# A hybrid attention and gated-MLP layer in float32 splits: where squares, first loads, a gate and a residual are placed

## Chip, cores, metric

One core of one Trainium2 chip runs the whole layer in one launch. The metric is the device time of a run in microseconds (us), median over runs. TensorE is PE in the profile, VectorE DVE, ScalarE ACT, GpSimd POOL, and SyncE (SP) issues the DMAs.

## What is computed

One layer over 1024 positions of width 1024. `mod` comes from a small product of the conditioning vector and gives shift, scale and gate for both halves.

```python
h = modulate(rmsnorm(x, g_attn_norm[l]), sh_a, sc_a)
proj = jnp.dot(h, w_in[l])
...
o_mla = mla_attention(q, k, v)
...
o_ca = chunk_attention(cq, ck, cv, rel_bias[l])
mixed = jnp.dot(jnp.concatenate([o_mla, o_ca], axis=-1), w_out[l])
x = x + g_a[:, None, :] * mixed
h = modulate(rmsnorm(x, g_mlp_norm[l]), sh_m, sc_m)
u = causal_dwconv(jnp.dot(h, w_up[l]), conv_w[l], conv_b[l])
gate, val = jnp.split(u, 2, axis=-1)
x = x + g_m[:, None, :] * jnp.dot(jax.nn.silu(gate) * val, w_down[l])
```

All inputs are float32. `w_up` is 1024 x 5632 (gate and value columns), `w_down` 2816 x 1024.

## The kernel before

**Splits.** To multiply float32 on TensorE each operand is split into a high part (a rounded copy, mostly by ScalarE, `hi_of`, L75) and a low part (operand minus high part, `lo_of`, L82, or L1098 for the up weights). A product is then three matmuls: high x high, high x low, low x high. Matmuls are 128 x 128 by 128 x 512.

**Order.** The kernel is written on a framework that places tiles in pools, sets the semaphores, and fixes each engine's order of instructions beforehand with estimated times: an instruction goes in when its inputs and its buffer are expected to be ready, earlier lines of the program first. At run time every engine, and SyncE's queue of DMA issues, goes strictly in that order. `tc.issue_after(ins)` puts the instructions of its block behind `ins` on the same engine.

**Attention (to about 695 us).** Scores, softmax and values of 32 units, with projections woven in as fillers. The last filler, `f_oca` (L689), takes the chunk attention's half of the output projection: for each half n of the columns it loads four blocks of `w_out` (`load_wo`, L677), splits them, and for eight tiles t of positions loads the attention output, multiplies (tile `oc`), copies PSUM to an SBUF tile `co` (L701, ScalarE) and stores it to `part_d` in DRAM. `co`, the raw blocks `wor` and others share two buffers ("sq"). `f_ada` (L503) makes the modulation vectors on the side; the attention gate, spread over 128 partitions, goes to `ga_d`.

**Output projection (about 695 to 785).** `load_wo` brings the other half's weights (L1022). First the up weights of tiles 0 and 1 are loaded and scaled (L1124 to L1127). Then for each t (L1129): load `ol`, split it (ScalarE, GpSimd), load x and the kept part `pa`, multiply (tile `op`), then on VectorE pa + op, times the gate row `gabc`, plus x (L1143 to L1145); x1 is stored to `x1_d`, squared (ScalarE), and scaled in place by its inverse root mean square (GpSimd for t < 4, else ScalarE). After t = 3 the first half of the positions is transposed and modulated (`mod_T`, L1048) and split into pages (`bpage`, L1056); the second half follows after the first products of tiles 0 and 1 (`ff_first`).

**Up stage (about 785 to 1259).** 22 tiles j of 128 gate and 128 value columns. The product of the two weight blocks with the two halves of the positions is done in seven products instead of eight, by sums and differences of blocks (`ff_w`, L1109, gives the split weights wa to wg in turn; `ff_tile`, L1195, multiplies and recombines in tile `c`). Each product is 12 matmuls in float16 parts; so that the parts keep within range, a tile's raw weights (`wu`, 8 buffers, four tiles) are first squared and summed on ScalarE (L1083), summed over partitions by TensorE (L1085), and scaled (L1093): `scale_ff`, L1078. `conv` (L1175) is the depthwise convolution: one ScalarE and two VectorE instructions each for gate and value; then SiLU, the product of both (L1222) and a store to `g_d` (L1223). The loop (L1272 on) calls for tile j: load of tile j+3, scaling of tile j+2, the seven products of j, and one step of `gate_row`, which makes the MLP gate `gmbc`.

**Down stage (from about 1259).** For each half h of the positions all eight PSUM banks hold 4 x 2 output tiles. The four x1 tiles are loaded (`xo`, L1308); for each j the block of `w_down` is loaded (`wd`), multiplied by the gate (L1313) and split, g is loaded (`gr`, L1316) and split, and 24 matmuls (L1323 to L1325) accumulate. At the end VectorE adds x1 (L1329) and the result is stored.

```python
    for j in range(NF):
        if j + 3 < NF:
            load_ff(j + 3)
        if j + 2 < NF:
            scale_ff(j + 2, bank("G", f"wss_ps{j + 2}"))
        ff_tile(j)
        if j >= 2:
            next(gate, None)
```

Of the kernel before, what the change touches and what calls it, by code (L numbers as in the profile page):

```python
# [12 lines left out]
F32 = mybir.dt.float32  # L13
# [49 lines left out]
def layer_kernel(ctx, tc, I, out):  # L63
# [9 lines left out]
    def hi_of(eng, o, i):  # L73
        if eng == "a":
            act.activation(o, i, AF.Copy)  # L75
        elif eng == "p":
            pool.tensor_scalar(o, i, 1.0, 0.0, op0=MUL, op1=ADD)  # L77
        else:
            dve.tensor_copy(o, i)
# [22 lines left out]
    pool.memset(nhalf[:], -0.5)  # L102
    modT = cst.tile([P, 4, ND], F32, name="modT")
# [399 lines left out]
    def f_ada():  # L503
        for m in (2, 3, 4):
            for n in range(4):
# [15 lines left out]
                if m == 2:  # L521
# [3 lines left out]
                    sp.dma_start(ga_d[:, n * 256:(n + 1) * 256], g[:])  # L525
                else:
# [150 lines left out]
    def load_wo(k0, n, he, le):  # L677
        ws = []
        for k in range(k0, k0 + 4):
            raw = qtile(f"wor{k}_{n}")  # L680
            sl = slice(n * 512, (n + 1) * 512)
            sp.dma_start(raw[:], I["w_out"][k * P:(k + 1) * P, sl])
            w = g4([P, 2, 512], F32R, f"wo{k}_{n}")
            hi_of(he, w[:, 0], raw[:])
            lo_of(le, w[:, 1], raw[:], w[:, 0])
            ws.append(w)
        return ws

    def f_oca():  # L689
        for n in range(2):  # L690
            ws = load_wo(4, n, "a", "p")
            for t in range(NT):
# [8 lines left out]
                act.activation(o[:], pt[:], AF.Copy)  # L701
# [230 lines left out]
    ca_done = []  # L932

# [131 lines left out]
    gabc = gb.tile([P, D], F32, name="gabc")  # L1065
    sp.dma_start(gabc[:], ga_d[:])


    raws, wsc = {}, {}
# [8 lines left out]
    def scale_ff(j, pt):  # L1078
        t = cst.tile([P, 4], F32, name=f"wss{j}", tag="wss", bufs=3)
        sv = cst.tile([P, 2, 4], F32, name=f"wcv{j}", tag="wcv", bufs=3)  # L1080
        for i in range(2):
            junk = xp.tile([P, D], BF16, name=f"wj{i}_{j}", tag="wj", bufs=1)
            act.activation(junk[:], raws[j][i][:], AF.Square, accum_out=t[:, i:i + 1])  # L1083
        for i in range(2):
            pe.matmul(pt[:, 0:1], ones[:], t[:, i:i + 1], start=(i == 0), stop=(i == 1))  # L1085
        dve.tensor_scalar(t[:, 2:3], pt[:, 0:1], 1.0 / VSCALE ** 2, 1e-20, op0=MUL, op1=ADD)
        pool.tensor_tensor(t[:, 2:3], t[:, 2:3], nhalf[:], op=ALU.pow)
        dve.reciprocal(t[:, 3:4], t[:, 2:3])
# [6 lines left out]
    def split(src, nm):  # L1095
        w = mt("ws", [P, 2, 512], nm, F16)
        hi_of("a", w[:, 0], src)
# [30 lines left out]
    gens = {}  # L1128
    for t in range(NT):  # L1129
        lo = gb.tile([P, 4, P], F32R, name=f"ol{t}", tag="ol", bufs=3)  # L1130
        hi = gb.tile([P, 4, P], F32R, name=f"oh{t}", tag="oh", bufs=3)
        sp.dma_start(f32(lo[:]), oT_d[0:4, :, t * P:(t + 1) * P].rearrange("k p t -> p k t"))
        hi_of("a", hi[:], f32(lo[:]))
        lo_of("p", lo[:], f32(lo[:]), hi[:])
        x1 = tb.tile([P, D], F32, name=f"x1_{t}", tag="x1", bufs=8)
        sp.dma_start(x1[:], I["x"][t * P:(t + 1) * P, :])
        pa = gb.tile([P, D], F32, name=f"pa{t}", tag="pa", bufs=3)
        sp.dma_start(pa[:], part_d[t])
# [8 lines left out]
        act.activation(pa[:], x1[:], AF.Square, accum_out=ss2[:, t:t + 1])  # L1147
        rsqrt_mean(r2[:, t:t + 1], ss2[:, t:t + 1], D)
        xn2[t] = x1
        if t < 4:  # L1150
            scale_pool(x1[:], x1[:], r2[:, t:t + 1])
        else:
# [41 lines left out]
    def ff_tile(j):  # L1194
# [28 lines left out]
        sp.dma_start(g_d[j], ug[:])  # L1223

    w0 = [next(gens[0]) for _ in range(2)]
# [19 lines left out]
    tbp.__exit__(None, None, None)  # L1245
# [159 lines left out]
```

## Time and profile before

| | |
|---|---|
| median of 3 runs | 1528.38 us (1525.49 to 1531.11) |
| profiled execution | 1528.33 us, its span 1526.6 us |
| mean granted TensorE clock | 0.939 |
| busy share of the span | PE 87%, DVE 69%, ACT 53%, POOL 47% |
| moved by DMA | 153.05 MB, mean 100 GB/s |

The span runs from the first to the last instruction on the core. A row of the timeline gives start (us), duration, engine, line, operation, tiles written and read, shapes, count, and in brackets the idle time before it with what ended it. A row of waits gives who waited for whom, us in total, times, and the longest. The letter q behind an engine's name means its queue, "x8" that eight instructions are merged. A matmul's duration includes its fill; the distance between two starts is what it costs in a row of many.

### The profile page before, as it was taken

The numbers are of one execution on the slowest core, as the hardware profiler recorded it, in microseconds if no ns is written. First come the engines' busy times: TensorE is split into PE (matmuls) and PEld (weight loads), VectorE is DVE, ScalarE is ACT, GpSimd is POOL, SyncE is SP. The second block draws the span as 40 slices with busy tenths as digits, with TensorE's granted clock in tenths as the row PEclk, the third lists the DMA queues.
The fourth block names the chain that finished last, engine by engine and source line by source line (L and its number), as shares of the span: only waits on it lengthen the run. The fifth ranks groups of instructions, "written<-read, shape, count | busy, mean of one in ns | idle before, by whom it ended". The sixth has DMA issues, their size and how long they took to land. (4 is left out here: it accounts for less than half of the span.)

```text
span 1526.6 us, 20386 instructions
## 1 busy us (share of the span) xinstructions
PE 1328.3 (87%) x7016; PEld 902.0 (59%) x7016; DVE 1054.8 (69%) x1721; ACT 814.7 (53%) x1537; POOL 717.3 (47%) x753
## 2 busy tenths in 40 slices
PE   3779999988888899977879899888898994999999
PEld 2679878867655466645634344433344443888887
DVE  8856776665898755575459986786777975656654
ACT  5445565455777677666277654555456422333332
POOL 5543342333353433224722865554555623665764
PEclk9879999999889899988889999999999996999999
DMA  8322123211100133228332322211221006445442
GB/s 304 107 81 64 55 83 107 82 56 44 54 22 12 49 94 99 82 63 310 112 138 76 118 84 83 83 70 55 83 81 44 39 32 264 142 146 198 153 147 96
DMA packets 82308, 153.05 MB, mean 100 GB/s; under 512 B 8470, under 2 KB 44570, under 8 KB 82204
## 3 DMA queue, kind: packets, MB, share of 16 engines
q1 hardware_dynamic: 82204, 151.75, 29.6%
q8 instruction: 55, 0.90, 0.2%
q14 instruction: 49, 0.40, 0.1%
HBM read 122.88 MB, written 28.84 MB: 99 GB/s over the span
## 5 line engine op out<-in xcount | busy, mean ns | idle before, releaser
L82 POOL TENSOR_TENSOR wds<-wd,wds 128x512 fp32r<-128x512 f32 x88 | 156.0, 1792 | 118.9 <-ACT wds L75 118.9
L1323 PE MATMUL dn<-wds,g 128*128 128x512 f32 x352 | 135.7, 395 | 22.1 <-ACT g L75 22.1
L75 ACT ACTIVATE wds<-wd 128x512 fp32r<-128x512 f32 x88 | 54.8, 624 | 164.9 <-PE dn L1325 146.6
L1324 PE MATMUL dn<-wds,g 128*128 128x512 f32 x352 | 136.5, 391 | 0.0
L1325 PE MATMUL dn<-wds,g 128*128 128x512 f32 x352 | 134.8, 389 | 0.0
L1313 DVE TENSOR_TENSOR wd<-wd,gmbc 128x1024 f32<-128x1024 f32 x44 | 68.9, 1566 | 90.4 <-DMA wd<-w_down 90.4
L1083 ACT ACTIVATE wj<-wu 128x1024 bf16<-128x1024 f32 x44 | 46.4, 1054 | 110.4 <-DMA wu<-w_up 103.4
L1177 ACT ACTIVATE u<-c,pk,wcv 128x1024 f32<-128x1024 f32 x44 | 52.1, 1232 | 70.4 <-DVE c L1217 49.6
L1323 PEld LDWEIGHTS dn<-wds,g 128*128 128x128 f32 x352 | 67.1, 191 | 36.7 <-ACT g L75 22.6
L515 DVE SCALAR_TENSOR_TENSOR aacc<-aw,cs,aacc 128x256 f32<-128x256 f32 x84 | 45.2, 538 | 56.6 <-DMA aw<-w_ada 56.2
L82 DVE TENSOR_TENSOR g<-gr,g 128x512 fp32r<-128x512 f32 x44 | 72.8, 1655 | 12.4 <-ACT g L75 12.3
L839 PE MATMUL tm<-qt,kt 96*128 96x512 f16 (+7 forms) x288 | 75.3, 351 | 6.2 <-ACT qt L802 3.6
L850 DVE TENSOR_TENSOR hlm<-pm,hlm 128x512 f16<-128x512 f32 (+1 forms) x96 | 55.2, 581 | 36.8 <-ACT hlm L847 18.9
L1098 POOL TENSOR_TENSOR wd<-wu,wd 128x512 f16<-128x512 f32 x22 | 40.4, 1835 | 85.1 <-issue 66.5
L1324 PEld LDWEIGHTS dn<-wds,g 128*128 128x128 f32 x352 | 66.7, 189 | 13.8
L1325 PEld LDWEIGHTS dn<-wds,g 128*128 128x128 f32 x352 | 66.2, 188 | 13.8
L843 ACT ACTIVATE pc<-tc,sca 128x512 f32<-128x512 f32 (+3 forms) x96 | 49.9, 522 | 38.3 <-DVE hlc L850 20.5
L77 POOL TENSOR_SCALAR hlm<-pm 128x384 f16<-128x384 f32 (+2 forms) x48 | 24.4, 509 | 97.2 <-ACT pm L843 74.8
L1121 DVE TENSOR_TENSOR wu<-wu 128x512 f32<-128x512 f32 x22 | 26.0, 1181 | 60.9 <-POOL wb L1098 60.6
L839 PEld LDWEIGHTS <-kt 128*128 128x128 f16 (+2 forms) x480 | 47.1, 102 | 35.2 <-issue 16.6
L1178 DVE SCALAR_TENSOR_TENSOR u<-c,wcv,u 128x1023 f32<-128x1023 f32 x44 | 57.4, 1340 | 12.2 <-ACT u L1177 12.2
L843 ACT ACTIVATE pm<-tm,scm 128x512 f32<-128x512 f32 (+1 forms) x96 | 55.2, 578 | 19.1 <-PE tm L839 15.3
(463 smaller groups left out, 4605.8 us busy)
## 6 DMA issues: line engine op xcount, KB each, us to landing
wu<-w_up SPq DMA_DIRECT2D x44, 512.0 KB, 3.8
wd<-w_down SPq DMA_DIRECT2D x44, 512.0 KB, 3.6
aw<-w_ada SPq DMA_DIRECT2D x96, 128.0 KB, 2.1
g_d<-u SPq DMA_DIRECT2D x22, 512.0 KB, 2.6
gr<-g_d SPq DMA_DIRECT2D x44, 256.0 KB, 3.7
x<-x SPq DMA_DIRECT2D x16, 512.0 KB, 10.1
adaw<-w_ada_a SPq DMA_DIRECT2D x16, 512.0 KB, 4.5
wq_r<-w_qk SPq DMA_DIRECT2D x32, 128.0 KB, 2.4
```

The source lines that it names most:

```text
L75: act.activation(o, i, AF.Copy)
L82: return (pool if eng == "p" else dve).tensor_tensor(o, i, f32(hi), op=SUB)
L839: last = pe.matmul(s[:, c0:c1], l, m, start=(y == 0), stop=(y == len(todo) - 1))
L843: act.activation(p[:, :w], s[:, :w], AF.Exp, scale=ninv)
L850: dve.tensor_tensor(hl[:, 1, :w], p[:, :w], hl[:, 0, :w], op=SUB)
L1083: act.activation(junk[:], raws[j][i][:], AF.Square, accum_out=t[:, i:i + 1])
L1177: act.activation(u[:], c, AF.Identity, scale=sv[:, 2:3], bias=pk[:, C_CV + 4 * ch + 3:C_CV + 4 * ch + 4])
L1178: dve.scalar_tensor_tensor(u[:, 1:], c[:, :S - 1], sv[:, 1:2], u[:, 1:], op0=MUL, op1=ADD)
L1313: dve.tensor_tensor(raw[:], raw[:], gmbc[:], op=MUL)
L1323: pe.matmul(pts[t][n], sh, w[n][:, 0], start=(j == 0), stop=False)
L1324: pe.matmul(pts[t][n], sh, w[n][:, 1], start=False, stop=False)
L1325: pe.matmul(pts[t][n], sl, w[n][:, 0], start=False, stop=(j == NF - 1))
```

## The change

It has five parts. (1) In the up stage a tile's weights are squared behind the last high part split so far, which is a tile two back, since `scale_ff` now follows `ff_tile`; the store of g of tile j-1 is issued in iteration j, behind the load of tile j+3; the square root's inverse and the root itself are both made by GpSimd. (2) The first three loads of `w_down` and of g are issued in the last three iterations of the up stage, into a pool of their own (`dna`), and the down stage's other buffers are opened in the up stage's place; its PSUM banks are taken in another order; x1 is loaded at steps 4 to 7; 3 buffers for gr instead of 5. (3) The gate of the attention is multiplied into the output weights, and the residual x is added in the kept part, so the output projection has one sum left. (4) In the output projection, four tiles' loads go first, the low part of `ol` and the scaling are VectorE's, and the first up weights are loaded and scaled between the tiles. (5) All pages of the first half have their low part made by VectorE.

```diff
+                    if n == 3:
+                        ga_done.append(1)
...
             sp.dma_start(raw[:], I["w_out"][k * P:(k + 1) * P, sl])
+            pool.tensor_tensor(raw[:], raw[:], gab[0][:, sl], op=MUL)
...
     def f_oca():
+        while not ga_done:
+            next(side[0])
+        gab.append(pgtile([P, D], F32, "gabc"))
+        sp.dma_start(gab[0][:], ga_d[:])
...
-                act.activation(o[:], pt[:], AF.Copy)
+                sp.dma_start(o[:], I["x"][t * P:(t + 1) * P, n * 512:(n + 1) * 512])
+                dve.tensor_tensor(o[:], o[:], pt[:], op=ADD)
                 sp.dma_start(part_d[t][:, n * 512:(n + 1) * 512], o[:])
...
+    def behind(x):
+        return tc.issue_after(x.ins) if x is not None else nullcontext()
...
-        for i in range(2):
-            junk = xp.tile([P, D], BF16, name=f"wj{i}_{j}", tag="wj", bufs=1)
-            act.activation(junk[:], raws[j][i][:], AF.Square, accum_out=t[:, i:i + 1])
+        with behind(last.get("hi")):
+            for i in range(2):
+                junk = xp.tile([P, D], BF16, name=f"wj{i}_{j}", tag="wj", bufs=1)
+                act.activation(junk[:], raws[j][i][:], AF.Square, accum_out=t[:, i:i + 1])
...
+        pool.tensor_tensor(t[:, 3:4], t[:, 2:3], phalf[:], op=ALU.pow)
         pool.tensor_tensor(t[:, 2:3], t[:, 2:3], nhalf[:], op=ALU.pow)
-        dve.reciprocal(t[:, 3:4], t[:, 2:3])
...
     def split(src, nm):
         w = mt("ws", [P, 2, 512], nm, F16)
-        hi_of("a", w[:, 0], src)
+        last["hi"] = hi_of("a", w[:, 0], src)
...
-    for j in range(2):
-        load_ff(j)
-    for j in range(2):
-        scale_ff(j, ps2.tile([P, 512], F32, name=f"wss_ps{j}", tag="hT", bufs=2))
+    def load_o(t):
+        lo = gb.tile([P, 4, P], F32R, name=f"ol{t}", tag="ol", bufs=4)
+        hi = gb.tile([P, 4, P], F32R, name=f"oh{t}", tag="oh", bufs=4)
+        sp.dma_start(f32(lo[:]), oT_d[0:4, :, t * P:(t + 1) * P].rearrange("k p t -> p k t"))
+        x1 = tb.tile([P, D], F32, name=f"x1_{t}", tag="x1", bufs=8)
+        sp.dma_start(x1[:], part_d[t])
+        o_hl[t] = hi, lo
+        xn2[t] = x1
+
+    for t in range(4):
+        load_o(t)
+        if t % 2:
+            load_ff(t // 2)
     for t in range(NT):
...
+        if t + 4 < NT:
+            load_o(t + 4)
...
-        lo_of("p", lo[:], f32(lo[:]), hi[:])
+        lo_of("v", lo[:], f32(lo[:]), hi[:])
...
-        dve.tensor_tensor(pa[:], pa[:], pt[:], op=ADD)
-        dve.tensor_tensor(pa[:], pa[:], gabc[:], op=MUL)
-        dve.tensor_tensor(x1[:], x1[:], pa[:], op=ADD)
+        dve.tensor_tensor(x1[:], x1[:], pt[:], op=ADD)
         sp.dma_start(x1_d[t], x1[:])
...
-        if t < 4:
-            scale_pool(x1[:], x1[:], r2[:, t:t + 1])
-        else:
-            act.activation(x1[:], x1[:], AF.Copy, scale=r2[:, t:t + 1])
+        dve.tensor_scalar(x1[:], x1[:], r2[:, t:t + 1], None, op0=MUL)
+        if t == 1:
+            scale_ff(0, ps2.tile([P, 512], F32, name="wss_ps0", tag="hT", bufs=2))
         if t == 3:
             for k in range(ND):
                 mod_T(k, 0, ps2, "hT", 2)
-                bpage("b11" if k < 4 else "b21", k % 4, hf[k, 0], "v" if k % 2 else "p")
-            gens[0] = iter(list(ff_w(0)))
+                bpage("b11" if k < 4 else "b21", k % 4, hf[k, 0], "v")
+            gens[0] = ff_w(0)
+            w0 = [next(gens[0]) for _ in range(2)]
+        if t == 4:
+            gens[0] = iter(list(gens[0]))
+            scale_ff(1, ps2.tile([P, 512], F32, name="wss_ps1", tag="hT", bufs=2))
...
-        sp.dma_start(g_d[j], ug[:])
+        gout.append((j, ug))
...
+    def store_g():
+        while gout:
+            j, ug = gout.pop(0)
+            sp.dma_start(g_d[j], ug[:])
...
+    def load_down():
+        h, j = steps[len(dl)]
+        raw = dna.tile([P, D], F32, name=f"wd{h}_{j}", tag="wd", bufs=3)
+        last["wd"] = sp.dma_start(raw[:], I["w_down"][j * P:(j + 1) * P, :])
+        gr = dna.tile([P, 512], F32, name=f"gr{h}_{j}", tag="gr", bufs=3)
+        sp.dma_start(gr[:], g_d[j][:, h * 512:(h + 1) * 512])
+        dl.append((raw, gr))
...
             load_ff(j + 3)
+        if j >= NF - 3:
+            load_down()
+        store_g()
+        ff_tile(j)
         if j + 2 < NF:
             scale_ff(j + 2, bank("G", f"wss_ps{j + 2}"))
-        ff_tile(j)
...
+        for t, n in ((0, 0), (0, 1), (1, 0), (3, 0), (3, 1), (1, 1), (2, 0), (2, 1)):
+            pts[t][n] = ps4.tile([P, 512], F32, name=f"dn{t}{n}_{h}", tag=f"d{t}{n}", bufs=1)[:]
...
+            if len(dl) <= h * NF + j:
+                load_down()
+            raw, gr = dl[h * NF + j]
...
+            if h == 0 and j == 0:
+                store_g()
+            if j in (4, 5, 6, 7):
+                t = j - 4
+                xo.append(dnb.tile([P, D], F32, name=f"xo{h}{t}", tag="xo", bufs=5))
+                with behind(last["wd"]):
+                    sp.dma_start(xo[t][:], x1_d[4 * h + t])
```

More of the change, by code (lines that the diff above doesn't have):

```diff
@@ L1 @@
 import math
-from contextlib import ExitStack
+from contextlib import ExitStack, nullcontext
 import numpy as np
@@ L102, in layer_kernel @@
     pool.memset(nhalf[:], -0.5)
+    phalf = cst.tile([P, 1], F32, name="phalf")
+    pool.memset(phalf[:], 0.5)
     modT = cst.tile([P, 4, ND], F32, name="modT")
@@ L932, in layer_kernel @@
     ca_done = []
+    ga_done = []
     def fill_step():
@@ L1222, in ff_tile @@
         dve.tensor_tensor(ug[:], ug[:], uv[:], op=MUL)
-        sp.dma_start(g_d[j], ug[:])
-    w0 = [next(gens[0]) for _ in range(2)]
+        gout.append((j, ug))
+    gout = []
+    def store_g():
+        while gout:
+            j, ug = gout.pop(0)
+            sp.dma_start(g_d[j], ug[:])
     ff_first(0, w0, "p27")
@@ L1270, in layer_kernel @@
     gate = gate_row()
+    dl = []
+    steps = [(h, j) for h in range(2) for j in range(NF)]
+    def load_down():
[5 more added lines that the diff above has]
+        dl.append((raw, gr))
     load_ff(2)
```

63 lines of the change are left out of this document (23 added, 40 removed).

## The prediction

> **What bounds the kernel now.** I read the stages first (busy time by stretch, cut where TensorE changes its work): 694.7 is the end of attention, 784.7 the second half of the transposes, 812.5 the first full tile of the up stage, 1258.7 its last product, 1280.8 the first product of the down stage. Columns: stretch, length, busy us (instructions) of PE, PEld, DVE, ACT, POOL, then granted clock, DMA share, GB/s.
>
> ```profile
> 694.70:716.80 22.10, 19.49 (x80) 15.45 (x80) 8.01 (x12) 12.26 (x20) 7.68 (x9) 0.92 0.93 350
> 716.80:735.40 18.60, 3.99 (x8) 1.83 (x8) 12.01 (x11) 9.82 (x17) 18.43 (x14) 0.57 0.62 226
> 735.40:784.70 49.30, 45.44 (x193) 31.32 (x194) 24.43 (x20) 23.03 (x37) 25.53 (x27) 0.89 0.36 128
> 812.50:900.00 87.50, 79.71 (x357) 35.87 (x357) 80.43 (x86) 57.18 (x84) 60.01 (x39) 0.94 0.32 106
> 900.00:1180.00 280.00, 250.19 (x1154) 114.29 (x1153) 199.00 (x194) 153.61 (x221) 142.46 (x114) 0.98 0.20 72
> 1180.00:1258.70 78.70, 74.65 (x333) 33.18 (x331) 65.19 (x56) 31.68 (x43) 38.91 (x29) 0.96 0.08 34
> 1258.70:1280.80 22.10, 0.02 (x1) 0.02 (x1) 9.61 (x8) 5.10 (x6) 1.04 (x1) 0.57 0.57 213
> 1280.80:1526.60 245.80, 242.00 (x1056) 199.88 (x1056) 146.69 (x103) 76.91 (x129) 154.91 (x88) 0.99 0.46 159
> ```
>
> The down stage is TensorE's own: 1056 matmuls in 245.8 us (0.233 each, tail included) at clock 0.99, so only what lies before it can be had. TensorE loses 14.6 us in one hole at 716.8, 22.1 between up and down, and in the up stage more than its busy time shows, because after each wait the clock is down for some us. The waits of the up stage (812 to 1260: total us, times, longest), then SyncE's own queue, and from the page's DMA issues the w_up loads (KB, median us to landing):
>
> ```profile
> ACT wj L1083 <- DMA wu<-w_up: 98.5, 26, 8.6
> DVE wu L1121 <- POOL wb L1098: 58.5, 14, 6.6
> PE p L1105 <- DVE c L1211: 29.1, 11, 4.0
> SPq L1223 <- DVE u L1222: 345.6, 22, 21.2
> ...
> wu<-w_up SPq DMA_DIRECT2D x44, 512.0 KB, 3.8
> ```
>
> The rows link into a ring, read from the last wait of PE back. The second product (L1211's p27 buffer is single) waits for VectorE; VectorE is late because L1121 sits ahead of L1217 and waits for GpSimd's low part of wb; that waits for ScalarE's high part; ScalarE stands in the squares of L1083, at the head of its queue, waiting for a weight load; and the load stands in SyncE's queue behind the store of g, which waits for the previous tile's last VectorE product L1222. The timeline shows the ring's pace.
>
> ```profile
> 1067.72 0.38 PE L1105 MATMUL p<-b,wg 128*128 128x512 f16 x1
> 1070.31 0.50 PE L1085 MATMUL wss_ps<-wss,ones 128*128 128x1 f32 x4
> 1070.67 0.38 PE L1105 MATMUL p<-b,wa 128*128 128x512 f16 x1
> ...
> 1071.37 1.58 POOL L1098 TENSOR_TENSOR wf<-wu,wf 128x512 f16<-128x512 f32 x1
> 1071.86 2.17 DVE L1222 TENSOR_TENSOR u<-u,u 128x1024 f32<-128x1024 f32 x1
> 1072.91 2.13 POOL L1098 TENSOR_TENSOR wg<-wu,wg 128x512 f16<-128x512 f32 x1
> 1075.01 1.15 POOL L1098 TENSOR_TENSOR wa<-wu,wa 128x512 f16<-128x512 f32 x1
> ...
> 1077.13 0.69 DVE L1117 TENSOR_TENSOR wu<-wu,wu 128x512 f32<-128x512 f32 x1
> ```
>
> A product of 12 matmuls takes 1070.31 - 1067.72 = 2.59 us (0.216 each) and the sums of squares 0.36, so a tile of seven products needs 7 x 2.59 + 0.36 = 18.5 us of TensorE. The stretch 900 to 1180 holds 1154 / 88 = 13.1 tiles, 21.35 us each: 2.85 lost per tile.
>
> **The change, part by part.**
>
> **Up stage: squares behind the last split, loads ahead of the store of g.** The squares of tile j+2 go behind the last high part of tile j, and g of tile j-1 is stored after the load of tile j+3 is issued. A load then has more than a tile (18 us) before its squares want it, against 3.8 us to landing: ScalarE's 98.5 us go. VectorE's reciprocal goes for a second power on GpSimd, off VectorE's queue. What is late next? TensorE's floor over 812.5 to 1258.7 is 1844 instructions, 80 of them sums: 1764 x 0.216 + 20 x 0.36 = 388 us against 446.2, so 58 is all there is. But VectorE and GpSimd hold each other up: L1222 above takes 2.17 under wf and wg, which take 1.58 and 2.13; alone they take:
>
> ```profile
> 1243.36 2.48 DVE L1178 SCALAR_TENSOR_TENSOR u<-c,wcv,u 128x1023 f32<-128x1023 f32 x2 [1.36 <-ACT u L1177]
> 1245.75 2.47 DVE L1179 SCALAR_TENSOR_TENSOR u<-c,wcv,u 128x1022 f32<-128x1022 f32 x2
> 1248.33 1.23 DVE L1222 TENSOR_TENSOR u<-u,u 128x1024 f32<-128x1024 f32 x1
> ...
> L1087 POOL TENSOR_TENSOR wss<-wss,nhalf x22: 542/554/1594, 712.3 to 1209.1; 128x1 f32<-128x1 f32 x22
> L1090 POOL TENSOR_SCALAR wcv<-pk,wss,h2inv x22: 348/1316/1868, 713.1 to 1218.3; 128x6 f32<-128x6 f32 x22
> ```
>
> The times fit turns: wf ends 1072.95, L1222 then runs its last 1.1 to 74.03, wg its last 1.0 to 75.04. Work that takes turns is, per tile, 2.48 + 2.47 + 1.23 + 4 x 0.69 = 8.9 on VectorE and 7 x 1.15 + 2 x 0.55 + 0.35 = 9.5 on GpSimd (one power more than now): 18.4, as much as TensorE's floor. Two queues that each wait for other things as well don't keep that full. Today's turns (one power less, 17.85) fill 84% of 21.35. Bounds: TensorE's floor (58 gained), and today's filling, 18.4 / 0.84 = 22.0 a tile (13 lost in 20 tiles). I take 19.9, a filling of 92%, about the middle of 84 and 100, since the ring's longest wait goes entirely: 1.45 x 20 tiles = 29 gained. The new pool for the down stage's first loads shifts the w_up buffers, so that some wait for pages of the second half to be made; that costs nothing while squares come a tile later, and one landing (3.8) if not.
>
> The Trainium skill (GPSIMD Engine Reference, Specifications) says that GpSimd's SBUF interfaces are shared with VectorE and contend with its instructions that have two SBUF inputs or a 2-port mode; the rows of wf, L1222 and wg agree. By that rule a denser tile only turns waiting for DMA into waiting for turns: rival 1.
>
> **Up to down.** The 22.1 us are a queue:
>
> ```profile
> 1267.58 0.32 SPq L1223 DMA_DIRECT2D g_d<-u  x1
> 1267.99 2.20 SPq L1308 DMA_DIRECT2D xo<-x_d  x4
> 1270.30 0.43 SPq L1312 DMA_DIRECT2D wd<-w_down  x1
> ...
> 1277.80 1.22 DVE L1313 TENSOR_TENSOR wd<-wd,gmbc 128x1024 f32<-128x1024 f32 x1 [10.24 <-DMA wd<-w_down]
> ...
> 1280.78 3.78 PE L1323 MATMUL dn<-wds,g 128*128 128x512 f32 x8 [22.12 <-ACT g L75]
> ```
>
> Now three wd and three gr (2.25 MB) are loaded in tiles 19 to 21, where DMA is 0.08 busy, into a pool of their own; wd x gate and the splits of the first two steps need only split buffers, which lie on raw buffers long read, so they fit before 1258.7. The four xo loads move to steps 4 to 7 behind a wd load. The new order of the output banks puts first those whose readers end early; the two under p34, last read by L1217, come in the fourth group. Removed: 22.1, and the cold start (8 matmuls in 3.78 instead of 1.86, about 2 in all). New cost: VectorE still does tile 21's chain (1.2 + 1.4 + 2.48 + 2.47 + 1.23, about 9 us) while step 2 must be ready two steps of 24 x 0.23 = 5.5 later, 11 us: a close fit. Bounds 16 to 24, taken 22. Fewer gr buffers (3 for 5): hidden by 16 us of products; without that cover each step would show part of a landing.
>
> **Output projection.** The hole at 716.8 and its reasons, with the new operations' prices:
>
> ```profile
> ACT oh L75 <- DMA ol<-oT_d: 24.6, 3, 16.5
> PE op L168 <- ACT oh L75: 13.0, 3, 8.9
> ...
> 700.46 9.41 SPq L1136 DMA_DIRECT2D x<-x  x8
> ...
> L82 POOL TENSOR_TENSOR ol<-ol,oh 128x512 fp32r<-128x512 f32 x8 | 10.2, 1281 | 10.0 <-ACT oh L75 9.9
> ...
> x_d<-x SPq DMA_DIRECT2D x8, 512.0 KB, 2.7
> ...
> L282 DVE TENSOR_SCALAR x<-x,rx x8: 741/753/786, 9.0 to 20.3; 128x1024 f32<-128x1024 f32 x8
> ```
>
> The fourth ol load was queued behind eight x loads (4 MB, DMA 0.93 busy). The change drops these 4 MB and the two weights' work ahead of the projection: four ol/part pairs come first, tile 0's squares after t = 1, tile 1's after t = 4. VectorE per tile: out go the product with the gate and one sum (each 128x1024 like L1222, 1.23 and more), in come a low part (0.69) and the scaling (0.75): less. GpSimd loses 1.28 and its four scalings, ScalarE its four. A new wait: the scaling overwrites x1 in place, so VectorE stands until x1's store has read it (2.7 us to landing; squares and power take 2 of them), with the next tile's low part behind it: up to 8 x 0.7 = 5. From 694.7 to 784.7 TensorE is busy 68.9 of 90.0, and the clock costs about 0.08 x 22.1 + 0.11 x 49.3 = 7: 21 + 7 = 28 to gain at most, and 8 if only the longest wait (8.9) goes. I take 20, nearer the upper end, since both reasons of the hole go (the late load and the early weights). The 27.8 us from 784.7 to 812.5, the transposes and pages of the second half, are not touched.
>
> **Attention.** The gate goes into 16 output weights and x into the kept part:
>
> ```profile
> L701 ACT ACTIVATE co<-oc x16: 592/597/603, 538.5 to 644.3; 128x512 f32<-128x512 f32 x16
> ...
> part_d<-co SPq DMA_DIRECT2D x16, 256.0 KB, 2.7
> ...
> L82 POOL TENSOR_TENSOR wo<-wor,wo x12: 1255/1272/1585, 518.2 to 655.7; 128x512 fp32r<-128x512 f32 x12
> ```
>
> 16 products of 1.27 on GpSimd, 16 adds of about 0.7 (as L1117) on VectorE for 16 copies of 0.6 on ScalarE, 16 loads of 256 KB on SyncE, and the gate's load moved here. A kept tile comes every 105.8 / 15 = 7.05 us, a store lands in 2.7, a load of that size about the same, two buffers: hidden. The first weights wait two or three GpSimd products longer: 0 to +4. Bounds -4 to +8, taken +1.
>
> **Sum**, against the profiled execution (1528.33, of which 1.7 outside the span; 0.05 under the median of the runs): 1528.3 - 29 - 22 - 20 + 1 = 1458.
>
> **The rivals.**
> 1. Turns bind. VectorE and GpSimd in turn set 21 us a tile: gain 7 in the up stage, 1528 - 7 - 22 - 20 + 1 = 1480. For: 18.4 of turns against 18.5, VectorE 80.4 of 87.5 busy in 812 to 900. Against: 199 of 280 later.
> 2. Nothing binds but TensorE: 50 gained in the up stage: 1437. For: ScalarE's 98.5 is by far the largest wait. Against: as above.
> 3. It doesn't do what it says: the planner puts the down stage's first splits behind tile 21's chain and the new ol loads still late, so those parts give 8 each: 1528 - 29 - 16 + 1 = 1484. For: engines run in an order fixed by estimates. Against: all their inputs are ready early.
> 4. Slower: the kept part. Load, add, store through two buffers, with VectorE's add ahead of attention's own subtractions. If a load goes out only when the store before has landed and the add stands for it, each tile shows 2.7 + 0.7 + 2.7 = 6.1: 16 x 6.1 = 98, 1528 - 70 + 98 = 1556. It decides from 70 / 16 = 4.4 us a tile. Against: 7.05 us a tile and two buffers.
>
> **Chances and range.** Forecast 0.57, rivals 0.17, 0.12, 0.10, 0.04. Likeliest 1458 on its own 1445 to 1472; the range takes in rivals 1 to 3 with some spread and half of the loss bound of the turns: 1432 to 1498. About 0.5% (8 us) is what a measurement tells from no change: faster 0.94, same 0.02, slower 0.04.
>
> **What would show it.** Right: no wait of L1083's squares for DMA, PE's wait for L1211 down from 29.1 to under 10, tile pitch near 19.9, first down matmul within 3 us of the last up product, transposes' second half near 765. Wrong: VectorE and GpSimd rows stretched to twice their lone time with pitch over 20.5; a hole before the first down matmul; kept-part tiles further apart than 7 us.

## The result, and the profile after

| | before | after |
|---|---|---|
| median of 4 runs | 1528.92 us (1525.49 to 1531.11) | 1451.13 us (1449.72 to 1454.53) |
| ratio to before, 95% interval | | 0.9496 [0.9471, 0.9522] |
| span of the profiled execution, granted clock | 1526.6 us | 1450.4 us, 0.959 |

The forecast was 1458 with a range of 1432 to 1498; the time came out 7 us below it. The terms behind it did less well. One execution further down, the profiled one of the kernel with the gate's product on VectorE (1688.6 us), ran at a granted clock of 0.744 against 0.93 to 0.97 in all others, so neither its time nor its stages are used.

The stages of the changed kernel, with the columns of the prediction's first fence. 707.30 is the first output-projection matmul, 754.50 the last, 802.50 the first add that closes an up tile (L1238), 1196.30 the last up product, 1205.50 the first down product.

```profile
530.00:707.30 177.30, 156.95 (x842) 99.63 (x842) 117.40 (x226) 105.75 (x193) 72.99 (x81) 0.93 0.33 104
707.30:754.50 47.20, 46.73 (x213) 37.99 (x214) 27.98 (x32) 26.45 (x46) 18.34 (x24) 1.00 0.64 237
754.50:802.50 48.00, 36.92 (x163) 17.74 (x162) 35.01 (x51) 33.49 (x55) 11.93 (x12) 0.89 0.20 63
802.50:900.00 97.50, 90.46 (x423) 41.62 (x422) 90.65 (x88) 60.01 (x85) 71.43 (x48) 0.98 0.46 156
900.00:1130.00 230.00, 230.00 (x1093) 107.69 (x1092) 197.08 (x177) 152.81 (x218) 148.51 (x127) 1.00 0.24 83
1130.00:1196.30 66.30, 66.30 (x311) 30.47 (x308) 53.94 (x48) 28.89 (x41) 33.00 (x27) 1.00 0.08 33
1196.30:1205.50 9.20, 0.07 (x1) 0.00 (x0) 7.32 (x7) 5.03 (x7) 1.01 (x1) 0.79 0.00 1
1205.50:1450.40 244.90, 241.13 (x1056) 199.03 (x1056) 150.43 (x101) 76.61 (x129) 151.38 (x88) 0.99 0.51 169
```

From 900 to the last up product TensorE is never idle (230.00 of 230.00, 66.30 of 66.30), at clock 1.00: 1093 / 88 = 12.42 tiles in 230 us are 18.52 us a tile, the floor of 18.5. The output projection is full too (46.73 of 47.2). One hole is left, the 9.2 us at 1196.3. The waits of all engines in the up stage (812 to 1196), the longest first:

```profile
ACT wd L75 <- DVE wu L1129: 80.6, 19, 7.8
POOL wss L1099 <- DVE wss L1098: 53.5, 17, 35.3
POOL wd L1110 <- ACT wd L75: 50.2, 19, 4.7
...
PE p L1117 <- DVE c L1232: 4.3, 3, 2.2
```

ScalarE's squares no longer wait for a weight load (98.5 us before); what it and GpSimd wait for now is time that they have to spare. TensorE's wait for VectorE's add went from 29.1 to 4.3. The same stage by groups of one line, engine and operation, 900 to 1100, first of GpSimd, then of VectorE (busy us, mean ns of one):

```profile
L1110 POOL TENSOR_TENSOR wa<-wu,wa 128x512 f16<-128x512 f32 x11 | 18.0, 1641 | 31.2 <-ACT wa L75 31.2
...
L1110 POOL TENSOR_TENSOR wf<-wu,wf 128x512 f16<-128x512 f32 x11 | 12.8, 1160 | 0.0
...
L1243 DVE TENSOR_TENSOR u<-u,u 128x1024 f32<-128x1024 f32 x11 | 23.9, 2174 | 0.0
...
L1238 DVE TENSOR_TENSOR c<-c,p 128x1024 f32<-128x1024 f32 x11 | 13.4, 1221 | 10.8 <-PE p L1119 10.5
```

The turns are there: L1243 takes 2.17 in every tile against 1.23 alone, and the low part wa (wb and wc alike) 1.64 against wf's 1.16. But they do not stop TensorE. Where the span got shorter, us, each from the fences above and the prediction's rows:

| stretch | before | after | difference | forecast |
|---|---|---|---|---|
| start to first output-projection matmul | 696.7 | 707.3 | +10.6 | +1 |
| to the first closing add of an up tile | 119.8 | 95.2 | -24.6 | -20 |
| to the last up product | 442.2 | 393.8 | -48.4 | -29 |
| hole before the down stage | 22.1 | 9.1 | -13.0 | -22 with the cold start |
| down stage | 245.8 | 244.9 | -0.9 | in the line above |
| span | 1526.6 | 1450.4 | -76.2 | -70 |

So four sizes were off, in both directions, and the experiments ask each of them why.

### The profile page after: what moved, and what is told of

Same layout as the page of the kernel before. It is cut to its first block, busy times and chain, and to the rows that moved or that the text cites. A ratio compares the mean times of both kernels' runs of the same rounds, so it can differ in the third digit from the quotient of the medians.

```text
span 1450.4 us, 20343 instructions
## 1 busy us (share of the span) xinstructions
PE 1308.1 (90%) x7016; PEld 896.4 (62%) x7016; DVE 1064.8 (73%) x1719; ACT 803.0 (55%) x1517; POOL 723.0 (50%) x776
## 4 chain that ended last, share of the span: by engine, by line
PE 57%; DVE 17%; DMA 11%; ACT 5%; issue 4%; POOL 4%; SPq 0%; DVEq 0%; POOLq 0%; ACTq 0%
PE p L1118 7%; PE p L1117 7%; PE p L1119 7%; DMA aw<-w_ada 7%; PE dn L1359 6%; PE dn L1361 5%; PE dn L1360 5%; PE tm L850 3%; DVE aacc L516 2%; DVE adaw L385 2%; DMA wor<-w_out 1%; DVE mz L806 1%; PE tc L850 1%; PE pvm L876 1%; DVE hlc L861 1%
## 5 line engine op out<-in xcount | busy, mean ns | idle before, releaser
L81 POOL TENSOR_TENSOR wds<-wd,wds 128x512 fp32r<-128x512 f32 x88 | 152.4, 1751 | 103.6 <-ACT wds L75 103.6
L1346 DVE TENSOR_TENSOR wd<-wd,gmbc 128x1024 f32<-128x1024 f32 x44 | 74.3, 1692 | 79.3 <-DMA wd<-w_down 79.3
L850 PE MATMUL tm<-qt,kt 96*128 96x512 f16 (+7 forms) x288 | 78.3, 357 | 8.5 <-ACT pm L854 4.6
L850 PEld LDWEIGHTS <-kt 128*128 128x128 f16 (+2 forms) x480 | 47.2, 103 | 40.0 <-issue 22.7
L861 DVE TENSOR_TENSOR hlc<-pc,hlc 128x256 f16<-128x256 f32 (+3 forms) x96 | 53.5, 562 | 13.1 <-ACT hlc L858 9.0
L1110 POOL TENSOR_TENSOR wa<-wu,wa 128x512 f16<-128x512 f32 x22 | 35.2, 1599 | 52.2 <-ACT wa L75 52.1
L850 PE MATMUL tc<-qt,kt 128*128 128x512 f16 (+3 forms) x192 | 56.6, 317 | 4.2 <-ACT pc L854 2.1
```

The costliest lines, as they stand in the source:

```text
L81: return (pool if eng == "p" else dve).tensor_tensor(o, i, f32(hi), op=SUB)
L850: last = pe.matmul(s[:, c0:c1], l, m, start=(y == 0), stop=(y == len(todo) - 1))
L861: dve.tensor_tensor(hl[:, 1, :w], p[:, :w], hl[:, 0, :w], op=SUB)
L1346: dve.tensor_tensor(raw[:], raw[:], gmbc[:], op=MUL)
```

## The experiments

Marks of each profile in us from the start of the span (the rows by tile and line give them): the first and last of the reciprocal chain's logarithms of attention's second part (rim), the first output-projection matmul, the first closing add, the end of the last up product, the first down product; they are good to 0.1 us. Times are medians; the ratio is to the kernel before on the same chip.

| kernel | time | ratio [95%] | rim first, last | proj. | add | last up | down | span |
|---|---|---|---|---|---|---|---|---|
| before | | | 470.4, 694.7 | 696.7 | 816.5 | 1258.7 | 1280.8 | 1526.6 |
| after | 1451.1 | 0.9496 [0.9471, 0.9522] | 474.0, 705.4 | 707.3 | 802.5 | 1196.4 | 1205.5 | 1450.4 |
| e1_ring_alone | 1479.5 | 0.9694 [0.9665, 0.9722] | 470.3, 691.7 | 693.6 | 812.5 | 1207.3 | 1229.7 | 1474.7 |
| e2_store_at_once | 1450.9 | 0.9482 [0.9464, 0.9499] | 470.3, 703.7 | 705.7 | 800.9 | 1194.8 | 1203.9 | 1448.9 |
| e3_squares_early | 1502.2 | 0.9817 [0.9802, 0.9832] | 473.3, 701.2 | 703.2 | 798.5 | 1244.2 | 1253.4 | 1499.2 |
| e4_part3_undone | 1450.3 | 0.9496 [0.9467, 0.9526] | 471.0, 698.5 | 700.5 | 804.0 | 1197.9 | 1207.0 | 1452.3 |
| e5_residual_late | 1456.4 | 0.9539 [0.9513, 0.9564] | 471.1, 704.6 | 706.6 | 805.6 | 1199.4 | 1208.5 | 1454.8 |
| e6_first_splits | 1441.6 | 0.9438 [0.9416, 0.9461] | 470.0, 702.9 | 704.9 | 799.8 | 1196.5 | 1196.1 | 1445.2 |
| e8_low_twice | 1578.6 | 1.0321 [1.0296, 1.0346] | 475.2, 706.8 | 708.7 | 812.4 | 1325.7 | 1336.8 | 1582.2 |
| e9_two_steps | 1445.6 | 0.9446 [0.9432, 0.9460] | 474.4, 703.8 | 705.7 | 801.0 | 1199.9 | 1199.5 | 1443.0 |
| e10_gate_dve | 1447.2 | 0.9473 [0.9441, 0.9505] | | | | | | |
| e11_second_behind | 1439.9 | 0.9423 [0.9400, 0.9445] | 469.3, 699.6 | 701.5 | 796.6 | 1193.3 | 1192.9 | 1437.3 |
| e11_again | 1441.3 | 0.9431 [0.9404, 0.9458] | 471.8, 700.1 | 702.1 | 797.4 | 1192.4 | 1192.1 | 1436.5 |
| e12_third_buffer | 1441.0 | 0.9431 [0.9404, 0.9457] | 471.8, 701.5 | 703.4 | 799.0 | 1194.0 | 1193.6 | 1437.8 |

**The ring alone (e1).** Part 1 of the diff on the kernel before, nothing else.

```diff
-        if j + 2 < NF:
-            scale_ff(j + 2, bank("G", f"wss_ps{j + 2}"))
+        store_g()
         ff_tile(j)
+        if j + 2 < NF:
+            scale_ff(j + 2, bank("G", f"wss_ps{j + 2}"))
...
-        for i in range(2):
+        with behind(last.get("hi")):
+            for i in range(2):
```

> The kernel before with part 1 alone: squares behind the last high part two tiles back, sums of squares after the tile's products, g stored one tile later, the second power. Everything else is as before. Theory A (with the ring cut only TensorE binds in the up stage): tile pitch about 18.5 us between 900 and the last product, the stage from the first p34 add to the last product falls from 442 to 392-400, the time to 1478-1486. Rival B (VectorE and GpSimd hold each other to a pitch near 19.9 when nothing else is changed, and part of the 48 us came from other edits): stage 412-420, time 1498-1507. Attention and the 22 us hole before the down stage stay as before under both.

The stage takes 1207.3 - 812.5 = 394.8, the time 1526.7 (the kernel before on that chip) - 1479.5 = 47 less: theory A. The windows of this kernel, columns as above:

```profile
900.00:1130.00 230.00, 230.00 (x1093) 107.64 (x1092) 199.43 (x178) 150.46 (x217) 148.68 (x126) 1.00 0.24 86
...
1207.20:1229.70 22.50, 0.10 (x2) 0.03 (x1) 9.50 (x8) 5.10 (x6) 1.04 (x1) 0.62 0.58 211
```

The same full 230 us as with the whole change, and the old hole of 22.5 behind it: the up stage's gain is all part 1's, and it does not touch the hole.

**Which half of part 1 (e2, e3).** First the store of g put back behind its own tile.

```diff
-        store_g()
         ff_tile(j)
+        store_g()
```

> The changed kernel with one half of the ring's cut undone: g is stored right after its tile instead of one tile later, so the store stands in SyncE's queue ahead of the next weight load and waits there for VectorE's last product of the tile. The squares stay behind the last high part. Theory A (squares that come late are enough: a load has a tile's time to land either way): up stage 394-398, time 1449-1455. Rival B (the store in front of the load is what made the load late): stage 410 or more, time 1467 or more, with ScalarE's squares waiting for the weight load again.

Nothing changes, and the reason is not the one that A gives: every engine's queue holds the same instructions in the same order as in the changed kernel. The planner places the store by its own estimates, so this line of the diff moves nothing. The run serves as a second profile of the same program: spans of 1450.4 and 1448.9, the first projection matmul at 707.3 and 705.7. The kernel before has the stores in the same place as well: in its trace and in the changed kernel's, SyncE has issued five stores of g ahead of the first load of tile 10's weights, sixteen ahead of tile 21's, and the same number in both for every tile between. So in the changed kernel a store still stands in front of each of these loads, and the up stage loses nothing by it. Then the squares:

```diff
-        with behind(last.get("hi")):
+        with nullcontext():
...
+        if j + 2 < NF:
+            scale_ff(j + 2, bank("G", f"wss_ps{j + 2}"))
         ff_tile(j)
-        if j + 2 < NF:
-            scale_ff(j + 2, bank("G", f"wss_ps{j + 2}"))
```

> The changed kernel with the other half undone: the squares of tile j+2 are issued ahead of tile j's products with nothing that holds them behind its splits, as before; g is still stored one tile later. Theory A (the squares at the head of ScalarE's queue are the ring's main link): up stage 415-442, time 1472-1500, ScalarE's squares wait for the weight load some 40-100 us. Rival B (with the store out of the way the load is early enough, wherever the squares stand): stage 394-400, time 1450-1457.

The stage takes 445.7, all of the gain is gone, and a little more (442.2 before; both this and the time of 1502.2 lie just over theory A's ranges). The longest waits of this kernel from 812 to 1244, and what its loads wait for in SyncE's queue:

```profile
ACT wj L1095 <- DMA wu<-w_up: 94.7, 29, 7.1
POOL wd L1110 <- ACT wd L75: 58.8, 17, 5.5
...
SPq L1086 <- POOL wf L1110: 138.3, 16, 19.6
```

94.7 us of ScalarE standing in squares for a load, as the 98.5 before: the ring is back whole. What part 1 gains is the place of the squares; the second power, which this kernel keeps, gains nothing by itself here. The last row shows how the ring closes: a load waits for GpSimd's low part wf, which reads the weights in the buffer that the load is to fill; GpSimd waits for ScalarE's high part, and ScalarE stands in the squares until a load has landed. In the kernel before it is the same: between 900 and 1180, eleven of the twelve first loads of a tile go out when a wf ends, 1.3 to 4.5 us after the store of g in front of them.

**How hard the turns bind (e8).** Every low part of the up weights is written twice; the second write repeats the first.

```diff
-        pool.tensor_tensor(w[:, 1], src, w[:, 0], op=SUB)
+        for _ in range(2):
+            pool.tensor_tensor(w[:, 1], src, w[:, 0], op=SUB)
```

> The changed kernel with each low part of the up weights computed twice on GpSimd (the second write is the same value), 7 x 1.15 = 8 us more GpSimd work per tile and none on the other engines. Theory A, as in the prediction's rival 1 and in its filling factor (VectorE and GpSimd work in exclusive turns): 8.9 + 17.5 = 26.4 us per tile, stage from 394 to about 550, time about 1605. Theory B (their instructions only stretch where they overlap, so that GpSimd's own sum of 17.5 is under TensorE's 18.5): stage 394-420, time 1450-1477.

The stage takes 513.2, between the two and nearer to A: (513.2 - 393.8) / 20 = 6.0 more a tile, 24.5. This kernel's busy times from 900 to 1100, columns as above:

```profile
900.00:1100.00 200.00, 167.21 (x719) 73.04 (x720) 149.91 (x113) 96.33 (x138) 187.75 (x140) 0.93 0.20 64
```

GpSimd first, then VectorE with both inputs in SBUF, then with one in PSUM (busy us, mean ns of one):

```profile
L1111 POOL TENSOR_TENSOR wf<-wu,wf 128x512 f16<-128x512 f32 x17 | 28.1, 1651 | 0.0
...
L1200 DVE SCALAR_TENSOR_TENSOR u<-c,wcv,u 128x1023 f32<-128x1023 f32 x16 | 30.1, 1918 | 19.9 <-ACT u L1199 19.9
...
L1239 DVE TENSOR_TENSOR c<-c,p 128x1024 f32<-128x1024 f32 x8 | 9.7, 1211 | 0.8 <-PE p L1120 0.8
```

GpSimd is the bound (187.75 of 200). Alone its work would be 17.5 a tile, under TensorE's 18.5; it takes 24.5 because VectorE's instructions push it out. So theory B falls: the turns are real and cost wall time once GpSimd is the longest. But they are not the plain sum either: the 8.9 + 17.5 = 26.4 of turns went through in 24.5, so some 2 us a tile overlap, where the prediction filled only 92% of a tile with turns. For the changed kernel, with 7 x 1.15 = 8.05 less, that leaves 24.5 - 8.05 = 16.4 us a tile, an estimate, and it lies 2 under TensorE's floor.

**The hole before the down stage (e6, e9, e11).** In the changed kernel wd x gate is done early, yet ScalarE's splits of it come last. VectorE's product, then ScalarE and TensorE there:

```profile
1170.57 4.44 DVE L1346 TENSOR_TENSOR wd<-wd,gmbc 128x1024 f32<-128x1024 f32 x3
...
1185.71 1.06 ACT L1242 ACTIVATE u<-u 128x1024 f32<-128x1024 f32 x1 [2.19 <-DVE u L1200]
1197.80 2.37 ACT L1198 ACTIVATE u<-c,pk,wcv 128x1024 f32<-128x1024 f32 x2 [11.03 <-DVE c L1238]
1202.84 1.06 ACT L1242 ACTIVATE u<-u 128x1024 f32<-128x1024 f32 x1 [2.67 <-DVE u L1200]
1203.80 1.13 ACT L75 ACTIVATE wds<-wd 128x512 fp32r<-128x512 f32 x2
1204.84 0.62 ACT L75 ACTIVATE g<-gr 128x512 fp32r<-128x512 f32 x1
...
1205.51 3.42 PE L1359 MATMUL dn<-wds,g 128*128 128x512 f32 x8 [9.14 <-ACT g L75]
```

The data lie ready at 1175.0 (1170.57 + 4.44), ScalarE idles 11 us from 1186.8, and the splits stand behind the SiLU of tile 21. The first step's split buffers are now taken from another pool that stays open:

```diff
-        w = dnb.tile([P, 2, 512], F32R, name=nm, tag="dws", bufs=7)
+        w = dnb.tile([P, 2, 512], F32R, name=nm, tag="dws", bufs=7) if nm not in FIRST else mt("ra", [P, 2, 512], nm, F32R)
...
+    FIRST = ("wds0_00", "wds0_01", "g0_0")
```

> The changed kernel with the split buffers of the down stage's first step (two of w_down, one of g) taken from four buffers that are free since tile 1, instead of the down stage's own pool, which lies on the up stage's raw buffers. Theory A (the 9.2 us hole before the first down product is buffer space: the splits are placed behind the SiLU of tile 21 since their buffers come free only then): the hole falls to 0.5-3 us, time 1442-1446. Rival B (the hole is work: VectorE's and ScalarE's chain of tile 21 must run first whatever the buffers): it stays over 7, time 1449-1453. A third way: the earlier splits delay tile 21's weights on ScalarE, so that the last product comes 1-3 us later and half of the gain goes.

The splits move between tile 21's weight splits, and the first down product follows the last up product without a gap: theory A, with a ratio of 0.9438 against 0.9496. The third way came true in part as well: in this profile, the longest of the kernel's four executions, the last up product ends 396.7 us after the first closing add, 2.9 later than in the changed kernel. From 1180 to 1260 TensorE's waits are now

```profile
PE dn L1361 <- ACT g L75: 3.7, 1, 3.7
PE p L1117 <- DVE c L1232: 1.0, 1, 1.0
```

The first is the same wait one step later: a step of 24 matmuls covers 24 x 0.23 = 5.5 of the 9.1 us, and the second step's splits are still where they were. So the second step's buffers too (one more of the same four, two halves each from the gate row's):

```diff
-    FIRST = ("wds0_00", "wds0_01", "g0_0")
+    FIRST = ("wds0_00", "wds0_01", "g0_0", "wds0_10")
...
+    early = {n: Two(n) for n in ("wds0_11", "g0_1")}
```

> The kernel with the first down step's split buffers in free ones, and now the second step's too (one more of the four, and two in the gate row's buffers, whose rows are used up). Theory A (the 3.7 us wait that is left at the second step is again buffer space): it goes, the second and third step follow with less than 1 us, time 1437-1441. Rival B (the third step's splits, behind the last tile's chain on VectorE, ScalarE and GpSimd, are late by as much): a wait of 2-4 us moves to the third step, time 1440-1443. Rival C: six splits between tile 21's weights delay its products by over 1 us.

The down stage starts without a wait, and TensorE waits in the up stage instead (398.9 us from the first closing add to the last product, 5.1 more than in the changed kernel): rival C. Its only wait from 1160 to 1260:

```profile
PE p L1117 <- DVE c L1232: 3.1, 1, 3.1
```

Six splits in a row stand ahead of tile 21's own weights. Behind its last high part they would not:

```diff
-        hi_of("a", w[:, 0], src)
+        with behind(last["hi"] if nm in SECOND else None):
+            hi_of("a", w[:, 0], src)
...
+    SECOND = ("wds0_10", "wds0_11", "g0_1")
```

> The kernel with two down steps' splits in free buffers, and ScalarE's high parts of the second step held behind the last high part of tile 21, so that they no longer stand between its splits. Theory A (the 3.1 us that TensorE waited for VectorE's add of tile 21 came from the second step's work being wedged in ahead of it): the wait falls to about 1, TensorE goes over to the down stage without a wait over 1, time 2 us under the two-step kernel, 1438-1443. Rival B (VectorE is late for tile 21 with one step's splits as much as with two): the wait stays near 3.

> The kernel with two early down steps and the second's high parts behind, once more, to be set beside the one with a third buffer on the same chip and for a second profile of the same instruction order. Time 1438-1445; first output-projection matmul 701-708 (before it: 701.5).

TensorE's waits over the whole transition, in the second of the two profiles:

```profile
PE p L1117 <- ACT wds L75: 1.0, 1, 1.0
PE dn L1374 <- ACT g L75: 0.2, 1, 0.2
PE dn L1374 <- DVE c L1232: 0.2, 1, 0.2
```

1.4 us instead of 9.1. From the first projection matmul to the end it takes 735.8 and 734.4, against 743.1 and 743.2 in the two profiles of the changed kernel: 8 less. By the same measure e6 takes 740.3 and e9 737.3. Ratios of 0.9423 and 0.9431 lie clear of the changed kernel's 0.9496 and 0.9482. This version beats both kernels; e6, e9 and e11 are not told apart by their intervals.

**Part 3 (e4, e5, e10, e12).** Gate and residual back at the output, with ol, x and the weights' squares left where the change puts them:

```diff
-            pool.tensor_tensor(raw[:], raw[:], gab[0][:, sl], op=MUL)
...
-                sp.dma_start(o[:], I["x"][t * P:(t + 1) * P, n * 512:(n + 1) * 512])
-                dve.tensor_tensor(o[:], o[:], pt[:], op=ADD)
+                act.activation(o[:], pt[:], AF.Copy)
...
-        dve.tensor_tensor(x1[:], x1[:], pt[:], op=ADD)
+        dve.tensor_tensor(pa[:], pa[:], pt[:], op=ADD)
+        dve.tensor_tensor(pa[:], pa[:], gabc[:], op=MUL)
+        dve.tensor_tensor(x1[:], x1[:], pa[:], op=ADD)
```

> The changed kernel with gate and residual back in the output projection (no product of gate and output weights, kept part copied by ScalarE, three VectorE sums per tile at the output), but the ol and x loads still four tiles ahead and the up weights' squares still behind. Theory A (the 10 us that attention got longer are mostly this part's: the gate's product stands ahead of the splits of the output weights): first output-projection matmul falls from 707 to 697-702. Rival B (they are the order of the other edits, or spread from run to run): it stays at 705-708. For the stage from there to the first p34 add, now 95: if the late loads alone had made it 120, it stays at 95-100; if the three sums had, 105 or more. Time 1441-1447 if A holds and the sums cost nothing, 1451-1461 if the sums cost what A gives.

Attention's second part is read from one line's instructions: count, ns of one (min/median/max), first and last start. In the changed kernel its logarithms take 474.0 to 705.4, 231.4 us:

```profile
L883 ACT ACTIVATE rim<-pvm x16: 588/592/597, 474.0 to 705.4; 64x512 f32<-64x512 f32 x16
```

In e4 the same line's take 227.5:

```profile
L877 ACT ACTIVATE rim<-pvm x16: 589/592/596, 471.0 to 698.5; 64x512 f32<-64x512 f32 x16
```

Three profiles without the gate's product (before, e1, e4) give 221.4 to 227.5, mean 224.4; ten with it 227.9 to 233.5, mean 230.8: 6.4 us for the product and the earlier load of the gate that comes with it. Before and e1 lack other edits too, but the pair that differs only in where the gate is multiplied, e4 and e5 below, shows 6.0. Most of the remaining spread goes with the clock granted from 470 to 705: at 0.91 the part takes 227.5 without the product (e4) and 231.4 to 233.5 with it (after, e2, e5, e6), at 0.94 it takes 221.4 (e1) and 228.3 (e11_again). The part starts at 470.3 to 471.0 in the three and at 469.3 to 475.2 in the ten, in two profiles of the changed kernel's own order at 474.0 and 470.3: about 4 of the 10.6 us (474.0 against 470.4) are spread between runs. From the projection to the first closing add e4 takes 804.0 - 700.5 = 103.5 against 95.2: the two VectorE sums saved per tile, with the 4 MB of x that need no load there any more, are worth 8.3 there. The rest of that stage's gain, 119.8 - 103.5 = 16.3, comes from parts 4 and 5 together; how much the early loads have of it is not told apart. So part 3 gives some 8 and takes some 6, and the two times, 1450.3 and 1451.1, are the same.

Then only the residual back at the output:

```diff
-                sp.dma_start(o[:], I["x"][t * P:(t + 1) * P, n * 512:(n + 1) * 512])
-                dve.tensor_tensor(o[:], o[:], pt[:], op=ADD)
+                act.activation(o[:], pt[:], AF.Copy)
```

> The changed kernel with x added at the output again (kept part copied by ScalarE, no load of x into it, two VectorE sums per output tile), the gate still in the output weights. Theory A (the gate's product in front of the weight splits makes attention longer): first output-projection matmul stays at 705-708. Rival B (the kept part's load, VectorE add and store through two buffers do): it falls to 698-702. Stage from there to the first p34 add 95-99 if VectorE has room there.

Attention's part is as long as with it (233.5), so the kept part's load, add and store cost nothing there (theory A); at the output the one sum, with its loads, costs 99.0 - 95.2 = 3.8. What the product does in attention, by the waits from 480 to 710, of the changed kernel and then of e4:

```profile
POOL wor L686 <- DMA wor<-w_out: 10.5, 9, 2.7
ACT wo L75 <- POOL wor L686: 8.0, 9, 2.4
...
POOL wo L81 <- ACT wo L75: 7.6, 9, 1.9
ACT wo L75 <- DMA wor<-w_out: 5.9, 5, 1.7
```

With the product GpSimd, in whose queue attention's high parts stand, stops nine times for a weight load, and ScalarE, with attention's exponentials, nine times for GpSimd. Without it ScalarE waits for the loads, and GpSimd nine times for ScalarE: the same stops the other way round, some 5 us shorter in sum. That these stops make attention longer is not shown: in e5, which has the longest part of all (233.5), ScalarE waits only 2.7 us for GpSimd. Two ways out were tried on the kernels with early down steps. The product on VectorE (with the first step's splits):

```diff
-            pool.tensor_tensor(raw[:], raw[:], gab[0][:, sl], op=MUL)
+            dve.tensor_tensor(raw[:], raw[:], gab[0][:, sl], op=MUL)
```

> The kernel with the first down step's splits in free buffers, and the product of gate and output weights on VectorE instead of GpSimd (16 products of 128x512). In six profiles with the product on GpSimd the first output-projection matmul came at 703 to 709, with part 3 undone at 700.5, in kernels that keep the old attention at 694 to 697. Theory A (on GpSimd the product adds its 1.3 us ahead of each low part, in the queue that already does the low parts and the high-part copies of attention): the matmul falls to 697-702, time 1435-1440. Rival B (the length comes from the chain load, product, high part, low part through two buffers, wherever the product runs): it stays at 704-708, time 1441-1446. Rival C (VectorE is worse: its subtractions of attention wait): 709 or later.

1447.2 (0.9473) against 1441.6 (0.9438) with the product on GpSimd: theory A, 1435 to 1440, falls. The intervals of the two overlap, and whether B or C holds would need the stages; it stays open. And a third buffer (with two early steps):

```diff
-        return apg.tile([P, 512], F32, name=name, tag="sq", bufs=2)
+        return apg.tile([P, 512], F32, name=name, tag="sq", bufs=3)
```

> The kernel with two early down steps and the second's high parts behind, with three instead of two of the 128x512 buffers that the output weights pass through in attention (they are shared with the kept part and with attention's squares). Theory A (the gate's product costs 5 us in attention since GpSimd stands at it until the load of the weight has landed, with attention's own parts queued behind; a third buffer lets the load go out earlier): GpSimd's wait for that load falls from 10.5 to under 5 in total, the first output-projection matmul comes 3-5 us earlier than in the repeat without it, time 1434-1438. Rival B (the wait only moves, to the weights' split buffers or to another queue): within 2 us of the repeat.

The wait only moves: GpSimd's for the load falls to 8.9, ScalarE's for GpSimd grows to 12.3, and the first projection matmul comes at 703.4 against 702.1.

```profile
ACT wo L75 <- POOL wor L686: 12.3, 10, 2.7
POOL wor L686 <- DMA wor<-w_out: 8.9, 7, 3.5
```

That the product and what comes with it cost some 6 us is shown, by two profiles that differ in them alone and by the means; which of its links does, the wait for the load, the 16 instructions of 1.27 us or the longer chain, stays open.

## Why the prediction was right, and where it was not

**What bounds the kernel: right.** The ring of waits was the bound of the up stage. With the squares moved, the wait for DMA is gone and TensorE's wait falls as said (under 10; it is 4.3); with the squares moved back, all of it returns (e3). One link was misread: the load stands behind the store of g in both kernels, but what it waits for last is its buffer, which GpSimd's low parts still read (138.3 us in e3), and the diff's line for the store changes no order (e2).

**Up stage: cause of the gain right, the next limit wrong, size short by 19.** The term of 29 rested on 18.4 us of turns a tile, filled to 92%. The stretched rows came as foreseen, and e8 shows that turns bind when GpSimd has more to do. But the filling was mis-sized: the 84% from which it was taken came from a kernel whose engines also stood in the ring, and in e8 some 2 us a tile overlap, so by the estimate above the turns end at 16.4 and TensorE's floor of 18.5 decides: rival 2's price (50) for the up stage, and a pitch of 18.52 where 19.9 was foreseen. The Trainium skill (GPSIMD Engine Reference, Specifications) names the contention of VectorE instructions with two SBUF inputs; the rows agree: L1243 is at 2.17, and L1238, one of whose inputs is in PSUM, at 1.22 (1.21 in e8). The bound that the prediction built on the rule, rival 1, needed more GpSimd work than there is.

**Up to down: the step that failed.** The prediction says that "the splits of the first two steps need only split buffers, which lie on raw buffers long read, so they fit before 1258.7." They did not fit: 9.1 us were left of 22.1, and 13.0 gained of 22. The splits stood behind tile 21's chain, rival 3's mechanism for this one part, and its reason is the buffers: with others, nothing else changed, they move forward (e6). Why the planner holds that pool's buffers for taken until the chain's end stays open. The early loads themselves landed in time, as said.

**Output projection: right, 24.6 for 20.** Nearly all of the bound of 28 came. e4 splits it: 16.3 from parts 4 and 5, 8.3 from fewer sums and their loads; the prediction had counted the sums only as room on VectorE. The second half of the transposes starts at 763.2, foreseen near 765, but this mark says little: 8 of its 32 transposes now slip in between the first products, and the others follow from 771.3.

**Attention: outside its bounds.** Foreseen +1 between -4 and +8, measured +10.6. 4 of it is spread between runs, and the product's 6 or so lies inside the bound, but over the +4 that "two or three GpSimd products" at the first weights were to cost; through which link it does so stays open. The kept part, rival 4, costs nothing, though its tiles are 7.2 us apart, over the 7 that were to show it (they were 7.05 apart already): (651.8 - 544.0) / 15 by this row.

```profile
L712 DVE TENSOR_TENSOR co<-co,oc x16: 672/681/687, 544.0 to 651.8; 128x512 f32<-128x512 f32 x16
```

The total is near because 24 us gained beyond the terms (up stage, projection) met 18 of shortfall (transition, attention); that they nearly cancel is luck.

## What to carry to other kernels

Look first for an instruction that waits for a transfer at the head of a queue others feed from: moving two squares a tile was worth 47 us, more than all other edits together, with hardly any engine's work made less. When a hand-over between stages is meant to overlap, check the buffers as well as the data: a split whose inputs were ready 29 us early (1175.0 against 1203.8) stayed behind the old stage until it got buffers from a pool that was open. And a product folded into weights to save sums later is paid where the weights are made; count what that costs too (here some 6 for 8).

## What had not been expected of the hardware

Turns between VectorE and GpSimd stretch single instructions by 40 to 80% (1.16 to 1.64, 1.23 to 2.17), and in the changed kernel that costs nothing: TensorE is busy 230.00 of 230.00 us beside them. In e8 they cost 6.0 us a tile, though GpSimd's own sum of 17.5 us is still under TensorE's 18.5. Of VectorE's instructions in this stage those with both inputs in SBUF take part; those with one input in PSUM keep 1.21 to 1.22 us beside a GpSimd that is busy 94% of the time.
